# GpSimd arithmetic moved to VectorE in the Hyena and attention layers, and unsplit F32 side tasks in the first feed forward

## Chip, cores and metric

One core of a Trainium2 chip runs the whole program. The metric is the device time of one execution in microseconds, as the median of several runs. One more execution was taken by the hardware profiler, and every row below is from that one.

## What is computed

Two blocks follow each other on 256 tokens of width 1024, in F32. The first block has two layers; each is a hybrid mixer (stick-breaking attention, sparse attention with a top-k index, and a gated recurrence) and a feed forward of width 4096. The second block has two layers as well: a Hyena layer, an attention layer, each joined with a cross attention to a memory of 256 rows, and after each a mixture of 16 experts. Cut to the parts that the change touches:

```python
def second_block(x, mem, ...):
    mem_n = rms_norm_2(mem, mem_norm_g)
    for i in range(DEPTH):
        u = rms_norm_2(h, mix_norm_g[i])
        if i % N_MIXERS == 0:
            k_taps = hyena_filters(T, w1, b1, w2, b2, w3, freq)
            k_fft = jnp.fft.rfft(k_taps, axis=0)
            main = hyena_mixer(main_in, short_w, k_fft, skip)
        else:
            q = apply_axial_rope(rms_norm_2(q, at_q_norm_g[j]), cos, sin)
            kk = apply_axial_rope(rms_norm_2(kk, at_k_norm_g[j]), cos, sin)
            main = blocked_gqa(q, kk, vv)
        cross = memory_cross_attn(cq, mem_n, w_mem_kv[i])   # mem_n @ w_kv
        h = h + jnp.concatenate([main, cross], axis=-1) @ w_out[i]
        h = h + expert_choice_ffn(rms_norm_2(h, ffn_norm_g[i]), ...)
```

The Hyena filters (a small network with two sine layers, a third product with w3, a decay, a norm and a Fourier transform) and the memory's keys and values depend on no token, so the kernel makes them early, beside the first feed forward.

## The kernel before, in words

**Split products.** A weight tile or an activation is split into a high part (`hi`, rounded to F32R) and the rest (`lo`), and each product of two split operands is made of three F32R matmuls into one PSUM tile: `mm3`, lines 304 to 306. `split` (line 284) makes the parts of a weight tile: ScalarE copies `hi` (line 291), and the next engine of the cycle `lo_engines[0]` subtracts for `lo` (line 292). The cycle differs from stage to stage: VectorE alone in the mixers of the first block; `LO0 = (G, V)` in both feed forwards (`mlp`); `LO1 = (G, V)` in `hyena_layer`; `LO2 = (V, G, V)` in `attention_layer`, and `LO3 = (G, V)` for its output projection. `V` is VectorE, `S` ScalarE, `G` GpSimd, `PE` TensorE.

**Units and steps.** The dense work is a row of units (`dense_T`, `dense_M`, the closures in `mlp` and `out_second`). A unit first prepares (loads and splits a tile), two units ahead of its matmuls, and then runs: 24 matmuls of 256 columns or 12 of 512. `Pipe.feed` prepares and runs them in turn, and after each unit it takes every spawned task one step further, to its next `yield`. `Pipe.join` goes on until a given task has ended, with units as long as there are some. The instructions of each engine stand in one queue in an order that the framework's planner sets from its own costs.

**Weights.** `Ring.one` takes the next buffer and issues its transfer (line 187) on SP's queue. SP waits, in order, until the buffer's former content has been read. In the first block the ring has five buffers of 2048 elements a partition; later stages have other ones, and those of the experts become free as Hyena and attention release their own tiles.

**Side tasks of the first feed forward.** `mlp0_tasks` (line 1834) is spawned before `mlp(0, ...)` and joined before its last chunk. It runs `filters_task` (line 1063) and then `memory_task` (line 1161). `filters_task` makes `h1` and `h2` with `sin_layer`, keeps `h2` stacked as high and low part in `hst`, loads `w3` in four blocks, splits each block (`w3h`, `w3l`, line 1112 on GpSimd), makes two matmuls for each direction `d` (lines 1122 and 1123, of 128 and of 64 rows), multiplies by the decay (line 1124), sums absolute values on GpSimd (line 1130), makes sum and difference of the two directions, splits these (lines 1136 and 1137), and transforms them by `mm3` with the split Fourier matrix `Fh`, `Fl`. `memory_task` norms the memory with `Norm`, whose `half` (line 339) transposes on TensorE and splits the columns on ScalarE (line 347) and VectorE (line 348), and then makes keys and values for both layers by the helper `stream` over `dense_T` and `dense_M` units. These tasks end with 69 yields; the feed forward gives them some 62 units.

**Hyena.** `hyena_layer` (line 1309) feeds the projections `v`, `x1`, the cross query and `x2` (20 units), and spawns four tasks `chain(o, n)`: a Fourier transform, a complex product with the filter (lines 1371 to 1380; GpSimd has one of the two combinations, line 1375, and some of the `lo` parts), an inverse transform, and the gate. `short` (lines 1327 to 1334) makes the short convolution of a projection. `out_second` is the output projection, 16 units.

**Attention.** In `attention_layer` (line 1437), `rotate` multiplies by the sine table on GpSimd (line 1466) and by the cosine table on VectorE (line 1468). `attend` makes scores, softmax and values.

**Other lines named below.** 371 is the row norm's broadcast by matmul, from `nrb`; 801 and 1215 are F32 matmuls of the attentions; 1142 and 1143 are the filters' norm; 1352 is the transposition ahead of a Hyena chain; 360, 361 and 321 are small steps of a norm's inverse root on 128x2 elements.

```python
        S.activation(hi, src, AF.Copy)
        next(lo_engines[0]).tensor_tensor(lo, src, hi.bitcast(F32), op=ALU.subtract)
```

## Time and profile before

| what | value |
|---|---|
| runs: median (lowest to highest) | 1873.15 us (1870.21 to 1873.5) |
| the profiled execution: its time, its span | 1872.64 us, 1870.8 us |
| busy: TensorE matmuls, weight loads | 1628.8 us (87%), 1195.2 us (64%) |
| busy: VectorE, ScalarE, GpSimd | 985.2 us (53%), 676.6 us (36%), 315.1 us (17%) |
| moved by the transfers | 490.41 MB, mean 262 GB/s |

The span goes from the first to the last instruction. PE is TensorE (PEld its weight loads), DVE VectorE, ACT ScalarE, POOL GpSimd, SP the queue that issues nearly all transfers. L292 is line 292 of the kernel before. Shares of the whole span say little here, since the stages have different limits; so the rows below are by stage. Times in the views count from the span's start. Matmuls overlap, so that what one costs is read from the distance of two starts and not from its duration.

### The profile page before, as it was taken

Reading aid. Unit: us, or ns where it says so; the run is one execution under the profiler, and the core shown is the slowest. Engines: PE = TensorE matmul, PEld = TensorE weight load, DVE = VectorE, ACT = ScalarE, POOL = GpSimd, SP = SyncE. Lnnn points to the kernel's source line nnn. Section 1 sums busy time; section 2 is a strip of 40 time slices with the busy share of each in tenths; the row PEclk is TensorE's granted clock in tenths of the full one; section 3 lists DMA queues with packets and bytes.
Section 4 is the critical chain, followed back from the end, with each engine's and each line's share of the span. In section 5 each row is a group of like instructions: output and inputs, shape, how many; then the busy total and the mean of one; then the engine's idle time right before and its main releaser. Section 6 shows DMA issues by size and latency. Waiting matters only on the chain. (4 is left out here: it accounts for less than half of the span.)

```text
span 1870.8 us, 27208 instructions
## 1 busy us (share of the span) xinstructions
PE 1628.8 (87%) x11139; PEld 1195.2 (64%) x11139; DVE 985.2 (53%) x1740; ACT 676.6 (36%) x1118; POOL 315.1 (17%) x216
## 2 busy tenths in 40 slices
PE   8999999998999999999989988666667989776765
PEld 7998977788999989999878844212224655221221
DVE  6998686775579977645578752000006862110102
ACT  6446454554454555544445331000003652000001
POOL 1000026654300000444333300000002210000001
PEclk9999999999999999999999988898989999899888
DMA  7543564454644436755244689999998759999997
GB/s 257 160 137 125 172 201 160 164 203 161 209 142 147 130 124 203 278 185 196 99 153 157 254 353 425 425 426 424 426 405 315 272 203 401 425 425 425 425 421 274
DMA packets 136516, 490.41 MB, mean 262 GB/s; under 512 B 11153, under 2 KB 32068, under 8 KB 115912
## 3 DMA queue, kind: packets, MB, share of 16 engines
q1 hardware_dynamic: 135919, 488.11, 69.2%
q8 instruction: 87, 1.43, 0.3%
q10 hardware_dynamic: 472, 0.57, 0.1%
q14 instruction: 38, 0.30, 0.0%
HBM read 483.41 MB, written 5.24 MB: 261 GB/s over the span
## 5 line engine op out<-in xcount | busy, mean ns | idle before, releaser
L291 ACT ACTIVATE hi<-w 128x1024 fp32r<-128x1024 f32 (+3 forms) x330 | 328.0, 997 | 323.7 <-PE psT L306 162.3
L304 PE MATMUL psT<-xh,hi 128*128 128x256 f32 x1328 | 386.8, 291 | 0.9 <-ACT hi L291 0.9
L305 PE MATMUL psT<-xh,lo 128*128 128x256 f32 x1328 | 378.6, 285 | 4.6 <-POOL lo L292 2.7
L306 PE MATMUL psT<-xl,hi 128*128 128x256 f32 x1328 | 378.7, 285 | 0.0
L292 DVE TENSOR_TENSOR lo<-w,hi 128x1024 fp32r<-128x1024 f32 (+3 forms) x245 | 285.3, 1165 | 141.5 <-ACT hi L291 140.6
L292 POOL TENSOR_TENSOR lo<-w,hi 128x1024 fp32r<-128x1024 f32 (+1 forms) x85 | 205.0, 2413 | 590.2 <-ACT hi L291 584.6
L305 PEld LDWEIGHTS psT<-xh,lo 128*128 128x128 f32 x1328 | 256.4, 193 | 9.5 <-POOL lo L292 3.3
L304 PEld LDWEIGHTS psT<-xh,hi 128*128 128x128 f32 x1328 | 256.5, 193 | 9.2 <-issue 6.4
L306 PEld LDWEIGHTS psT<-xl,hi 128*128 128x128 f32 x1328 | 256.1, 193 | 1.4 <-issue 1.1
L1741 PE MATMUL psx<-w,late 128*32 128x256 f32 (+1 forms) x1024 | 154.4, 549 | 75.8 <-DMA w<-in_exp_w_gate 39.5
L1741 PEld LDWEIGHTS psx<-w,late 128*32 128x32 f32 x1024 | 47.1, 116 | 180.5 <-issue 74.9
L1741 PE MATMUL psx<-w,xg 128*32 128x256 f32 (+1 forms) x1024 | 124.3, 547 | 35.2 <-DMA w<-in_exp_w_up 19.7
L1793 PE MATMUL psy<-w,late 128*32 128x512 f32 x576 | 98.8, 601 | 33.7 <-DMA w<-in_exp_w_down 29.8
L1777 ACT ACTIVATE yy<-psy,rslot 128x512 fp32r<-128x512 f32 (+1 forms) x17 | 11.3, 662 | 320.6 <-PE psy L1793 253.7
L1741 PEld LDWEIGHTS psx<-w,xg 128*32 128x32 f32 x1024 | 40.5, 117 | 115.7 <-issue 60.6
L306 PE MATMUL acc<-lo,hh 128*128 128x512 f32 x256 | 100.8, 394 | 3.0 <-POOL lo L292 3.0
L305 PE MATMUL acc<-hi,hlo 128*128 128x512 f32 x256 | 100.8, 394 | 0.0
L304 PE MATMUL acc<-hi,hh 128*128 128x512 f32 x256 | 100.5, 392 | 0.0
L1778 DVE SCALAR_TENSOR_TENSOR yy<-psy,rslot,yy 128x512 fp32r<-128x512 f32 (+1 forms) x17 | 12.2, 720 | 162.0 <-ACT yy L1777 161.5
L1757 DVE TENSOR_TENSOR late<-late,psx 128x512 f32<-128x512 f32 (+1 forms) x16 | 8.1, 550 | 166.3 <-PE psx L1741 166.3
L1793 PEld LDWEIGHTS psy<-w,late 128*32 128x32 f32 x576 | 27.1, 110 | 101.1 <-DMA w<-in_exp_w_down 49.8
L1756 DVE SCALAR_TENSOR_TENSOR late<-psx,rslot,late 128x512 f32<-128x512 f32 (+1 forms) x16 | 9.1, 613 | 152.3 <-ACT late L1755 152.3
(495 smaller groups left out, 2850.1 us busy)
## 6 DMA issues: line engine op xcount, KB each, us to landing
w<-in_exp_w_gate SPq DMA_DIRECT2D x64, 1536.0 KB, 27.6
w<-in_exp_w_up SPq DMA_DIRECT2D x64, 1536.0 KB, 29.5
w<-in_exp_w_down SPq DMA_DIRECT2D x48, 1536.0 KB, 26.9
w<-in_w_in SPq DMA_DIRECT2D x39, 1024.0 KB, 5.2
w<-in_w_up SPq DMA_DIRECT2D x32, 1024.0 KB, 5.6
w<-in_w_down SPq DMA_DIRECT2D x32, 1024.0 KB, 7.1
w<-in_exp_w_down SPq DMA_DIRECT2D x18, 1024.0 KB, 14.2
w<-in_w_out SPq DMA_DIRECT2D x10, 1024.0 KB, 5.6
```

The source lines that it names most:

```text
L291: S.activation(hi, src, AF.Copy)
L292: next(lo_engines[0]).tensor_tensor(lo, src, hi.bitcast(F32), op=ALU.subtract)
L304: PE.matmul(ps, lh, rh, start=start, stop=False)
L305: PE.matmul(ps, ll, rh, start=False, stop=False)
L306: PE.matmul(ps, lh, rl, start=False, stop=stop)
L1741: mm = PE.matmul(pg[nm][n][32 * e:32 * e + 32, :c1 - c0], xg[gr // 2][:, k, 128 * (gr % 2) + 32 * e:128 * (gr % 2) + 32 * e + 32], wt[e][: ...
L1756: V.scalar_tensor_tensor(sg[:, :n], pg["gate"][i][:, :n], r2, sg[:, :n], op0=ALU.mult, op1=ALU.mult)
L1757: V.tensor_tensor(hid[:, c], sg[:, :n], pg["up"][i][:, :n], op=ALU.mult)
L1777: S.activation(yh, py, AF.Copy, scale=rs[:, 2, gr:gr + 1])
L1778: V.scalar_tensor_tensor(yl, py, rs[:, 2, gr:gr + 1], yh.bitcast(F32), op0=ALU.mult, op1=ALU.subtract)
L1793: PE.matmul(py[n][32 * e:32 * e + 32], hT[:, k, 32 * e:32 * e + 32], wt[e][:, k - k0, 512 * n:512 * n + 512], start=k == 0, stop=k == 5, t ...
```

## The change

The cycles `LO1`, `LO2` and `LO3` become VectorE alone, and the GpSimd instructions in `chain` and `rotate` go to VectorE; `LO0`, the cycle of both feed forwards, stays as it is. The side tasks use plain F32 operands in place of split ones: the memory's norm has a third form without `xl`; the memory's products read the weight tile of the ring; `filters_task` multiplies `h2` with `w3` by matmuls of 64 rows, one for each direction on its half of the rows, and transforms the unsplit sums.

```diff
@@ -277,9 +277,7 @@
     LO0 = (G, V)
-    LO1 = (G, V)
-    LO2 = (V, G, V)
-    LO3 = (G, V)
+    LO1 = LO2 = LO3 = (V,)
@@ -329,7 +327,10 @@
             self.src, self.g, self.ps = src, g, psum or B
-            if split:
+            self.x = None
+            if split is None:
+                self.x = pool.tile([128, 8, T], F32, name="xT")
+            elif split:
                 self.xh = (pool or xtp).tile([128, 8, T], F32R, tag="xh", name="xh")
@@ -344,6 +345,9 @@
                     k = k2 + j
+                    if self.x is not None:
+                        S.activation(self.x[:, k], ps[:, j], AF.Copy, scale=self.g[:, k:k + 1])
+                        continue
                     S.activation(self.xh[:, k], ps[:, j], AF.Copy, scale=self.g[:, k:k + 1])
@@ -1030,19 +1034,6 @@
...
-    def stream(units, pool):
...
@@ -1075,11 +1066,8 @@
             nc.sync.dma_start(dec, C["decay"])
-            raw = ring.one(C["fwd"]).rearrange("p t (s f) -> p t s f", s=2)[:, :, :, :128]
-            Fh = fp.tile([128, 2, 2, 128], F32R, name="fFh")
-            Fl = fp.tile([128, 2, 2, 128], F32R, name="fFl")
-            S.activation(Fh, raw, AF.Copy)
-            V.tensor_tensor(Fl, raw, Fh.bitcast(F32), op=ALU.subtract)
+            F = fp.tile([128, 2, 2, 128], F32, name="fF")
+            nc.sync.dma_start(F, C["fwd"].rearrange("p t (s f) -> p t s f", s=2)[:, :, :, :128])
             yield
@@ -1089,12 +1077,9 @@
             h2 = fp.tile([128, T], F32, name="fh2")
-            hst = fp.tile([128, T], F32R, name="fhst")
             ps = A("psf", [128, T])
...
             sin_layer(ps, fc[:, 1:2], fc[:, 2:3], h2, fp)
-            S.activation(hst, h2, AF.Copy)
-            V.tensor_tensor(hst[64:], h2[64:], hst[64:].bitcast(F32), op=ALU.subtract)
             ones = fp.tile([128, 2], F32, name="ones")
@@ -1103,25 +1088,22 @@
                     c = slice(384 * n, 384 * n + 384)
-                    w3 = fp.tile([128, 2, 384], F32, name="fw3")
+                    w3 = fp.tile([128, 384], F32, name="fw3", bufs=2)
                     for d in range(2):
-                        nc.sync.dma_start(w3[64 * d:64 * d + 64], I["hy_filt_w3_2"][0].rearrange("k (o d c) -> k o d c", o=2, d=2)[:, o, :, c])
-                    w3h = fp.tile([128, 2, 384], F32R, name="fw3h")
-                    w3l = fp.tile([64, 2, 384], F32R, name="fw3l")
-                    S.activation(w3h, w3, AF.Copy)
-                    G.tensor_tensor(w3l, w3[:64], w3h[:64].bitcast(F32), op=ALU.subtract)
-                    hs = {op: [fp.tile([128, 2, 384], F32R, tag=f"h{op}{i}", name="hs") for i in range(2)] for op in (ALU.add, ALU.subtract)}
+                        nc.sync.dma_start(w3[64 * d:64 * d + 64], I["hy_filt_w3_2"][0].rearrange("k (o d c) -> k o d c", o=2, d=2)[:, o, d, c])
+                    hs = {op: fp.tile([128, 2, 384], F32, tag=f"h{op}", name="hs") for op in (ALU.add, ALU.subtract)}
                     sab = fp.tile([128, 384], F32, tag="sab", name="sab")
...
                         hd = []
+                        sl = slice(t * 128, (t + 1) * 128)
+                        pd = [A("psf", [128, 384]) for _ in range(2)]
+                        for d in range(2):
+                            r = slice(64 * d, 64 * d + 64)
+                            PE.matmul(pd[d], h2[r, sl], w3[r], start=True, stop=True, tile_position=(64 * d, 0))
                         for d in range(2):
                             h = fp.tile([128, 384], F32, tag=f"hd{d}", name="hd")
-                            ps = A("psf", [128, 384])
-                            sl = slice(t * 128, (t + 1) * 128)
-                            PE.matmul(ps, hst[:, sl], w3h[:, d], start=True, stop=False)
-                            PE.matmul(ps, hst[:64, sl], w3l[:, d], start=False, stop=True)
-                            V.tensor_tensor(h, ps, dec[:, t, c], op=ALU.mult)
+                            V.tensor_tensor(h, pd[d], dec[:, t, c], op=ALU.mult)
                             if t == 0 and d == 0:
@@ -1131,10 +1113,7 @@
                         for op, dst in hs.items():
-                            x = fp.tile([128, 384], F32, tag="hx", name="hx")
-                            V.tensor_tensor(x, hd[0], hd[1], op=op)
-                            S.activation(dst[0][:, t], x, AF.Copy)
-                            G.tensor_tensor(dst[1][:, t], x, dst[0][:, t].bitcast(F32), op=ALU.subtract)
+                            V.tensor_tensor(dst[:, t], hd[0], hd[1], op=op)
                         yield
@@ -1147,7 +1126,7 @@
                         for t in range(2):
-                            mm3(pp[t], Fh[:, t, part], Fl[:, t, part], hs[op][0][:, t], hs[op][1][:, t], True, True)
+                            PE.matmul(pp[t], F[:, t, part], hs[op][:, t], start=True, stop=True)
                         S.activation(e, pp[0], AF.Copy)
@@ -1158,24 +1137,32 @@
-    def memory_task(ring, mp, sp, m, kvd):
-
-        nm = Norm(m, gain("mem_norm_g_2"), mp, A)
+    def memory_task(ring, mp, m, kvd):
+
+        nm = Norm(m, gain("mem_norm_g_2"), mp, A, None)
         yield from nm.task(lambda n: True)
...
             yield
-
-            def put_k(j, ps):
-                V.tensor_tensor(kv[:, 0], ps, nm.R[:, None, :].to_broadcast([128, 2, T]), op=ALU.mult)
-
-            def put_v(ps):
+            yield
+            ps = A("psT", [128, 2, T])
+            for i in range(2):
+                for q in range(2):
+                    for k in range(4):
+                        PE.matmul(ps[:, q], w[i][:, k, 128 * q:128 * q + 128], nm.x[:, 4 * i + k],
+                                  start=i == 0 and q == 0 and k == 0, stop=i == 1 and q == 1 and k == 3)
+                yield
+            V.tensor_tensor(kv[:, 0], ps, nm.R[:, None, :].to_broadcast([128, 2, T]), op=ALU.mult)
+            ps = [A("psM") for _ in range(2)]
+            for k0 in range(0, 8, 2):
                 for t in range(2):
-                    evac(kv[:, 1, t], ps[t][:, :256], t, nm.r[:, t:t + 1])
-
-            yield from stream(dense_T(ring, None, nm.xh, nm.xl, put_k, tiles=[x[:, :, :256] for x in w]), sp)
-            yield from stream(dense_M(ring, None, nm.xh, nm.xl, put_v, tiles=[x[:, :, 256:] for x in w]), sp)
+                    for k in (k0, k0 + 1):
+                        PE.matmul(ps[t][:, :256], nm.x[:, k, t * 128:(t + 1) * 128], w[k // 4][:, k % 4, 256:],
+                                  start=k == 0, stop=k == 7)
+                yield
+            for t in range(2):
+                evac(kv[:, 1, t], ps[t][:, :256], t, nm.r[:, t:t + 1])
             nc.sync.dma_start(kvd[l], kv)
@@ -1372,12 +1359,12 @@
                 V.tensor_tensor(a[3], pz[1], kf[:, f], op=ALU.mult)
-                G.tensor_tensor(a[0], a[0], a[1], op=ALU.subtract)
+                V.tensor_tensor(a[0], a[0], a[1], op=ALU.subtract)
                 V.tensor_tensor(a[2], a[2], a[3], op=ALU.add)
...
                     S.activation(yh[:, b], a[2 * part], AF.Copy)
-                    (G if part and not o else V).tensor_tensor(yl[:, b], a[2 * part], yh[:, b].bitcast(F32), op=ALU.subtract)
+                    V.tensor_tensor(yl[:, b], a[2 * part], yh[:, b].bitcast(F32), op=ALU.subtract)
                 yield
@@ -1398,7 +1385,7 @@
                     S.activation(ah[:, b], sz, AF.Copy)
-                    (V if n else G).tensor_tensor(al[:, b], sz, ah[:, b].bitcast(F32), op=ALU.subtract)
+                    V.tensor_tensor(al[:, b], sz, ah[:, b].bitcast(F32), op=ALU.subtract)
                     ready.add(("a", b))
@@ -1463,7 +1450,7 @@
                     for g in range(2):
-                        G.tensor_tensor(hx(rot[:, t, a:a + 64 * nh])[:, :, :, g], hx(qk[:, t, a:a + 64 * nh])[:, :, :, 1 - g],
+                        V.tensor_tensor(hx(rot[:, t, a:a + 64 * nh])[:, :, :, g], hx(qk[:, t, a:a + 64 * nh])[:, :, :, 1 - g],
                                         xhf(tg[:, j, t, 1])[:, None, :, g].to_broadcast([128, nh, 2, 16]), op=ALU.mult)
@@ -1833,12 +1820,12 @@
         yield from filters_task(ring, kd)
-        with tc.tile_pool(name="memp", bufs=1) as mp, tc.tile_pool(name="mems", bufs=3) as sp:
+        with tc.tile_pool(name="memp", bufs=1) as mp:
             m = mp.tile([128, 2, D], F32, name="mem")
...
                 yield
-            yield from memory_task(ring, mp, sp, m, kvd)
+            yield from memory_task(ring, mp, m, kvd)
     with ExitStack() as c1s:
```

## Rows read from the trace of the kernel before

**Rows 1.** By stage: length, busy PE, PEld, DVE, ACT, POOL; clock; DMA share; GB/s.
```profile
226.00:520.00 294.00, 276.03 (x1723) 242.20 (x1723) 199.58 (x256) 146.43 (x212) 136.36 (x75) 0.99 0.54 182
...
740.00:935.00 195.00, 194.99 (x1233) 176.39 (x1231) 109.30 (x126) 96.28 (x122) 77.76 (x33) 1.00 0.55 188
935.00:1084.00 149.00, 133.04 (x891) 121.47 (x890) 115.16 (x198) 67.79 (x130) 52.70 (x38) 0.98 0.56 201
1084.00:1405.00 321.00, 234.11 (x1577) 88.71 (x1577) 51.42 (x112) 29.08 (x55) 2.26 (x3) 0.91 0.99 412
1405.00:1545.00 140.00, 123.73 (x622) 79.48 (x626) 97.39 (x255) 70.75 (x165) 33.85 (x35) 0.93 0.69 259
```

**Rows 2.** Waits of TensorE, 226:520 us: in total, times, longest.
```profile
PE pst L344 <- DVE xl L348: 4.8, 1, 4.8
PE psf L304 <- DVE nrm L1143: 3.6, 4, 0.9
PE acc L306 <- POOL lo L292: 3.0, 4, 0.8
PE psf L1122 <- DVE fhst L1097: 2.1, 1, 2.1
PE psn L1142 <- POOL sab L1130: 2.1, 3, 0.9
PE psf L1094 <- ACT fh L1061: 2.0, 1, 2.0
```

**Rows 3.** Timeline of GpSimd, 936:948 us: start, duration, then the instruction.
```profile
936.12 4.96 POOL L292 TENSOR_TENSOR lo<-w,hi 128x1024 fp32r<-128x1024 f32 x2 [8.96 <-ACT hi L291]
```

**Rows 4.** Timeline of VectorE, 936:948 us.
```profile
936.54 2.19 DVE L360 TENSOR_TENSOR ms<-ss 128x2 f32<-128x2 f32 x1
938.77 2.33 DVE L361 TENSOR_SCALAR ms<-ms 128x2 f32<-128x2 f32 x1
...
941.41 0.16 DVE L321 TENSOR_TENSOR rt<-rh,nr 128x2 f32<-128x2 f32 x1
941.49 1.22 DVE L292 TENSOR_TENSOR lo<-w,hi 128x1024 fp32r<-128x1024 f32 x1
```

**Rows 5.** By ten us, columns as in rows 1.
```profile
260.00:270.00 10.00, 7.96 (x51) 7.17 (x51) 9.26 (x24) 5.40 (x7) 4.23 (x2) 0.83 0.50 145
...
950.00:960.00 10.00, 9.74 (x67) 9.54 (x67) 3.89 (x5) 2.92 (x4) 1.79 (x1) 0.83 0.64 206
```

**Rows 6.** Timeline of TensorE, 307.4:309.3 us: split products.
```profile
307.58 0.28 PE L306 MATMUL psT<-xl,hi 128*128 128x256 f32 x1
307.70 0.34 PE L1122 MATMUL psf<-fw3h,fhst 128*128 128x384 f32 x1
307.97 0.44 PE L1123 MATMUL psf<-fw3l,fhst 64*128 64x384 f32 x1
...
309.07 0.38 PE L304 MATMUL psT<-xh,hi 128*128 128x256 f32 x1
```

**Rows 7.** Timeline of TensorE, 667.8:668.5 us: an unsplit product.
```profile
667.91 0.60 PE L801 MATMUL psz<-skbd,sqT 128*128 128x256 f32 x2
668.34 0.27 PE L802 MATMUL psz<-future_eqb,negI 128*128 128x256 bf16 x1
```

**Rows 8.** Timeline of TensorE, 1465:1466 us: products on halves of the columns.
```profile
1464.94 1.09 PE L1215 MATMUL psv<-pT,mvv 128*64 128x256 f32 x8
1465.96 0.39 PE L304 MATMUL psM<-hi,xh 128*128 128x256 f32 x1
```

**Rows 9.** Waits of TensorE, 935:1084 us.
```profile
PE psr L371 <- DVE nrb L366: 3.3, 1, 3.3
...
PE pst L1352 <- DVE uv L1334: 2.6, 2, 1.9
...
PE psT L305 <- POOL lo L292: 1.3, 1, 1.3
```

**Rows 10.** Waits of TensorE, 1405:1545 us.
```profile
PE psT L305 <- POOL lo L292: 1.4, 1, 1.4
```

More of the change, by code (lines that the diff above doesn't have):

```diff
@@ L1031, in wait @@
             yield
-    def stream(units, pool):
-        ahead = deque()
-        for u in units + [None, None]:
-            if u:
-                hl.append(pool)
-                u.prep()
-                hl.pop()
-                ahead.append(u)
-            if len(ahead) == 3 or not u:
-                ahead.popleft().run()
-            yield
     def sin_layer(ps, b, fr, out, pool):
```

## The prediction

> **What bounds the kernel now.** I read the profile in five steps. First the busy times by stage [rows 1]. The reader is to see four kinds of stage. From 226 to 520 us (output projection and feed forward of the first layer, with the side tasks) TensorE is busy 276 of 294 us: its work is time, and 18 us are holes. From 740 to 935 us (the second feed forward) it is busy 194.99 of 195 us. In Hyena (935 to 1084 us) and around attention (1405 to 1545 us) TensorE has 16 us of holes in each, and VectorE is busy 115 of 149 and 97 of 140 us. In the experts between them the transfers are busy 0.99 of the time.
>
> Second, who ended TensorE's waits in the first feed forward [rows 2]: VectorE, GpSimd and ScalarE, six groups, 17.6 us. Third, why these engines are late [rows 3, 4]: GpSimd makes two differences of 128x1024 from 936.12 us on, 2.5 us each, and VectorE's two instructions on 128x2 elements that fall into them take 2.19 and 2.33 us; one on 128x2 after them, at 941.41, takes 0.16. VectorE makes a difference of 128x1024 itself in 1.22 us. So GpSimd's arithmetic is not beside VectorE's: in those 4.96 us it stopped VectorE's queue, which is in order, for some 4.2. Fourth, the clock [rows 5]: 0.83 granted from 260 to 270 us, just after the wait on fh, is 3.4 us of ten at 1.2 instead of 2.4 GHz, 1.7 us of work lost; 0.83 stands in Hyena too, at 950 to 960 and again in the next ten, and 0.86 at 430 to 440 after the wait on xl. Fifth, what a product costs on TensorE [rows 6, 7], used below.
>
> **The change, part by part.**
>
> *Side tasks, TensorE.* A split product is three instructions; one of 256 columns starts 0.12 us after the one before [rows 6], so the product costs 0.36 us. An unsplit one in F32 is two instructions in the trace: the 256-column pair at 667.91 holds TensorE until 668.34, 0.43 us [rows 7]. Unsplit costs more here, by 0.07 us. Memory keys and values are 2 layers x 32 products: 64 x 0.07 = **+4.5 us**. The filters' Fourier products are 16 of 384 columns, each 1.5 x 0.36 = 0.54 split and 1.5 x 0.43 = 0.65 unsplit: 16 x 0.11 = **+1.8**. The w3 products now take 1.37 us for four instructions (307.70 to 309.07 [rows 6]), 8 x 1.37 = 11.0: 128 and 64 rows alternate, and an instruction costs 0.37 where its columns alone are 0.18. Afterwards they are 16 unsplit products of 64 rows, in pairs on the two halves of the rows. One after another: 16 x 0.65 = 10.4, and eight changes of the row count at 0.19, 1.5: 11.9, a loss of 0.9. Side by side: 5.2 + 1.5 = 6.7, a gain of 4.3. The nearest row has products on two halves of the columns: eight such instructions of 256 columns take 1.02 us [rows 8], where eight on the whole array take 4 x 0.43 = 1.7. So I take **-4.3**. TensorE's work: +2.0 us.
>
> Two rules bear on these terms. The Trainium skill, "FP8 and Floating Point Precision", TensorE Precision Notes, says that true FP32 takes four passes through the array. By it, at 0.12 us a pass, the memory part would be +7.7 and not +4.5; the measured pair, 0.43 instead of 0.48, decides. The Trainium skill, "TensorE: Matmul & The Clock Gate", in the table under "Why this matters for your kernels", says that matmuls on distinct row groups run concurrently. By it the w3 pairs would come out at the lower end; no row of this trace shows row groups.
>
> *Side tasks, waits* [rows 2]. The units of this stage keep their cycle of GpSimd and VectorE, so GpSimd goes on stopping VectorE; only the side tasks' own arithmetic leaves both. L344 on xl (4.8): the memory norm's VectorE half disappears, ScalarE alone frees the PSUM tiles and is next late: 4.8 gone. L1122 on fhst (2.1): this copy and difference are gone, h2 is ready at once: 2.1. acc on GpSimd's lo (3.0) and psn on sab (2.1): the sum stays on GpSimd and so does lo, but no w3l and no hs queue before them, nor before ScalarE's single buffer of absolute values: I take two thirds, 3.4. L1094 on fh (2.0): the sine's chain is stopped by one w3l, which goes, and by lo's, which stay: half, 1.0. nrm (3.6): its instructions stay: 0. Gone: 4.8 + 2.1 + 3.4 + 1.0 = 11.3, and 1.7 for the slow stretch of the clock after the wait on xl; the one after fh I keep. Nothing new comes to VectorE or ScalarE here.
>
> *Side tasks, queues.* The steps fall from 69 to 63 yields, against some 62 units; a step with no unit over it is matmuls either way: 0. SP issues one transfer for F instead of a ring tile, and w3 in half the bytes with two buffers, where it waited for GpSimd's fw3l. The memory weights stay in the ring until matmuls have read them, and these wait for the landing itself, two steps after the issue; TensorE's next unit is queued behind them, SP's next weights behind the two ring tiles. SP runs tiles ahead, so I take 0; the bound is a step for each layer, a unit of 24 x 0.12 = 2.9 us: +5.8.
>
> First feed forward: 2.0 - 11.3 - 1.7 = **-11.0 us**. Ends: -18, if 2.6 of nrm, the rest of the 17.6 and both slow stretches go (2.0 - 2.6 - 14.0 - 3.4); +6.1, if only xl and fhst go (6.9), w3 runs in series (5.2), both landings are late (5.8) and both slow stretches stay (2.0 - 6.9 + 5.2 + 5.8).
>
> *Second feed forward.* Not touched by the diff, and without a hole in TensorE [rows 1]: **0**.
>
> *Hyena.* GpSimd's 52.7 us [rows 1], nearly all arithmetic (10 lo, 8 hl, 15 smaller), become half of that, 26 us, on VectorE. In return its stops go: 0.85 of GpSimd's time in the head (4.2 of 4.96), and I estimate 0.4 over the stage, since not every VectorE instruction is stopped: 21 us. VectorE's load so goes from 115 to 120 of 149; what changes is that the row-norm and short-convolution chains no longer stand still. Of [rows 9] I count nrb (3.3), GpSimd's lo (1.3) and the longest of uv (1.9) as gone, and two slow clocks (3.4); I add 1 for the load: 3.3 + 1.3 + 1.9 + 3.4 - 1 = **-9** (ends -14 and 0). The experts' transfers start as Hyena frees its tiles and then run at 0.99; a shorter Hyena moves them forward whole.
>
> *Attention.* GpSimd has 29 of its 33.9 us to give (two memsets and the router stay): 14 on VectorE, 12 of stops less by the same 0.4. The wait on lo goes (1.4 [rows 10]); eight hl differences enter the softmax part, where they may hold its reductions up. I take **-1** (-4 to +4).
>
> Sum: -11.0 + 0 - 9 - 1 = -21.0. The profiled execution took 1872.6 us (span 1870.8 and 1.8 around it), 0.5 under the median of the runs. 1872.6 - 21.0 = **1851.6 us**.
>
> **Rivals.** *Only the side tasks pay.* VectorE in Hyena swaps stops for work of its own, and the holes come back behind other instructions. For: its load falls by nothing in my own sum. Against: the 128x2 instructions stand in the row-norm chain that TensorE waits for [rows 4, 9]. 1872.6 - 11.0 = 1861.6 us.
>
> *The unsplit products eat the side tasks' gain.* With w3 in series (5.2) and late landings (5.8) the side tasks come to -11.0 + 11.0 = 0; with -10 from Hyena and attention 1862.6 us. For: unsplit is dearer by the rows [rows 6, 7]. Against: the memory weights' landing has the ring's lead.
>
> *Slower: VectorE becomes the bound in Hyena and attention.* If its instructions are long for another reason than GpSimd, nothing is given back: Hyena needs 115 + 26 = 141 us of VectorE, at the present share of 77% a stage of 183, +34; attention 97 + 14 at 70%, 159, +19. Half of that where chains wait, +26, less 11.0: 1888 us. It decides once VectorE's load in Hyena passes the 133 us for which TensorE is busy. For: TensorE waits there mostly on VectorE [rows 9]. Against: two elements in a row cannot take 2.19 us by themselves [rows 4].
>
> *It doesn't do what it says.* The waits may move to other instructions in the new order of the queues; the second feed forward shows GpSimd doing no harm where TensorE is full. +2.0 for the products and some 4 us of waits less: 1871 us, no change.
>
> **Numbers.** Chances: the forecast 0.60; only the side tasks 0.14; the gain eaten 0.12; no change 0.07; slower 0.07. 0.2% is 3.7 us, about what a measurement can tell. Faster by more: 0.60 + 0.14 + 0.12 = 0.86; within: 0.07; slower: 0.07. The range goes from the three lower ends together (-18 - 14 - 4 = -36, 1837) past the second and third case (1862) to 1866, a little short of the side tasks' upper end with Hyena and attention as forecast (6.1 - 10 = -3.9, 1868.7), which needs every miss at once.
>
> **What would show it.** Right: TensorE's waits from 226 to 520 us fall to some 6 us, none on xl or fhst, while the side matmuls take some 2 us more; in Hyena no 128x2 instruction of VectorE takes over 0.3 us; Hyena ends some 20 us earlier than now. Wrong: the two w3 products of a pair start 0.6 us apart; TensorE waits for in_w_mem_kv; VectorE is over 90% busy through Hyena; or the expert stages grow by what was won before them.

## The result, and the profile after

The changed kernel takes 1830.5 us (median of 4 runs, 1829.9 to 1832.0), the kernel before beside it 1873.3 us: a ratio of 0.9776 (95% interval 0.976 to 0.9793), 42.8 us faster. The forecast was 21 us faster, and 1830.5 lies below its range. The profiled execution took 1830.5 us, of which 1828.7 are its span.

Three stages hold the gain; what lies ahead of them and between them changed by less than 1 us each. I measure each between two products that both kernels have: the first feed forward with its output projection from that projection's first product to the last product of the feed forward, Hyena from there (in the second layer) to its last output product, and the stretch from the first expert product to attention's first scores.

| stretch | before, us | after, us | difference | forecast |
|---|---|---|---|---|
| first feed forward | 277.1 | 257.3 | -19.8 | -11.0 |
| second feed forward | 204.8 | 204.9 | 0 | 0 |
| Hyena | 150.0 | 131.7 | -18.3 | -9 |
| experts to attention's scores | 375.2 | 368.9 | -6.3 | } -1 |
| the rest to the end | 394.5 | 395.8 | +1.3 | } |

The busy time by stage of the kernel after answers to [rows 1]; the columns are the same.

```profile
226.00:500.00 274.00, 272.68 (x1645) 236.02 (x1643) 172.60 (x241) 127.97 (x179) 95.81 (x49) 1.00 0.57 192
720.00:915.00 195.00, 194.98 (x1233) 176.50 (x1232) 112.03 (x126) 95.67 (x120) 77.75 (x33) 1.00 0.56 188
915.00:1046.00 131.00, 128.53 (x893) 118.17 (x892) 113.11 (x228) 68.54 (x129) 1.46 (x5) 1.00 0.64 229
1046.00:1363.00 317.00, 233.17 (x1572) 87.37 (x1570) 49.99 (x112) 28.21 (x54) 2.12 (x3) 0.91 0.99 412
1363.00:1503.00 140.00, 125.69 (x640) 78.89 (x636) 101.61 (x283) 71.88 (x167) 5.49 (x10) 0.92 0.73 272
```

TensorE's holes in the first stage fall from 18.0 to 1.3 us and in Hyena from 16.0 to 2.5, and the granted clock is 1.00 in both. In Hyena GpSimd goes from 52.70 to 1.46 us of work, all of it now VectorE's, and yet VectorE's busy time falls, from 115.16 to 113.11 us. In the first feed forward GpSimd keeps 95.81 us, the units' differences and the sums of absolute values.

TensorE's waits after, first from 226 to 500 us [rows 2], then from 915 to 1047 us [rows 9]: in total, times, longest.

```profile
PE psf L1129 <- DVE nrm L1122: 0.7, 1, 0.7
PE psr L375 <- DVE nrb L370: 0.3, 1, 0.3
PE psf L1081 <- ACT fh L1052: 0.3, 1, 0.3
...
PE pst L345 <- DVE X L998: 0.6, 1, 0.6
PE psy L302 <- ACT yh L1366: 0.5, 1, 0.5
```

Of the 17.6 us of [rows 2] 1.0 is left, on nrm and fh; the wait on nrb stood there before too, with the same 0.3. In Hyena no wait is over 0.6 us.

VectorE's timeline in Hyena's head shows why. The row-norm's two instructions that took 2.19 and 2.33 us beside GpSimd [rows 4] are these:

```profile
917.04 3.49 DVE L290 TENSOR_TENSOR lo<-w,hi 128x1024 fp32r<-128x1024 f32 x3
...
921.23 0.15 DVE L364 TENSOR_TENSOR ms<-ss 128x2 f32<-128x2 f32 x1
...
923.28 0.16 DVE L365 TENSOR_SCALAR ms<-ms 128x2 f32<-128x2 f32 x1
```

They take 0.15 and 0.16 us, and VectorE makes three differences of 128x1024 in 3.49 us, where GpSimd made two in 4.96 [rows 3].

The prices of products, from TensorE's timeline after: a pair of w3 products (its four records, then the next unit's first), and four unsplit memory products (eight records) with the two that follow.

```profile
300.36 0.92 PE L1103 MATMUL psf<-fw,fh 64*128 64x384 f32 x4
301.20 0.39 PE L302 MATMUL psT<-xh,hi 128*128 128x256 f32 x1
...
433.45 1.89 PE L1161 MATMUL psM<-w,xT 128*128 128x256 f32 x8
434.99 0.58 PE L302 MATMUL acc<-hi,hh 128*128 128x512 f32 x1
435.41 0.39 PE L303 MATMUL acc<-hi,hlo 128*128 128x512 f32 x1
```

A w3 pair holds TensorE from 300.36 to 301.20, 0.84 us, where the four split instructions of [rows 6] took 1.37. Four memory products take 1.54 us, and the split product behind them costs 0.42 instead of the usual 0.23: with that return, 0.43 us a product, what [rows 7] gave.

Around attention the waits on GpSimd's lo [rows 10], on cqT and on qp are gone, and these stand at the head of the list (1363 to 1503 us):

```profile
PE psM L302 <- ACT hi L289: 5.0, 1, 5.0
PE psa L1605 <- DVE aff L1602: 2.6, 1, 2.6
PE pss L1768 <- ACT yy L1764: 1.6, 2, 0.8
PE pst L1194 <- ACT p L785: 1.0, 1, 1.0
```

The first was 3.8 us before, and the two others that are gone were these:

```profile
PE psl L1197 <- DVE cqT L1546: 2.5, 1, 2.5
PE pst L1501 <- DVE qp L1493: 1.7, 2, 1.4
```

ScalarE's hi there starts behind the landing of attention's first weights, which queue behind the experts' transfers.

### The profile page after: what moved, and what is told of

It reads as the page before. It is cut to its first block, busy times and chain, and to the rows that moved or that the text cites. A ratio compares the mean times of both kernels' runs of the same rounds, so it can differ in the third digit from the quotient of the medians.

```text
span 1828.7 us, 26929 instructions
## 1 busy us (share of the span) xinstructions
PE 1617.8 (88%) x11059; PEld 1182.6 (65%) x11059; DVE 960.5 (53%) x1782; ACT 657.9 (36%) x1084; POOL 194.8 (11%) x132
## 4 chain that ended last, share of the span: by engine, by line
PE 60%; DMA 30%; DVE 6%; ACT 2%; issue 1%; SPq 1%; DVEq 0%; ACTq 0%
DMA w<-in_exp_w_up 10%; DMA w<-in_exp_w_gate 10%; DMA w<-in_exp_w_down 9%; PE psT L302 8%; PE psT L303 8%; PE psT L304 8%; PE acc L302 3%; PE acc L303 3%; PE acc L304 3%; PE psM L302 3%; PE psx L1728 3%; PE psM L303 2%; PE psM L304 2%; DVE lo L290 1%; SPq L187 1%
## 5 line engine op out<-in xcount | busy, mean ns | idle before, releaser
L289 ACT ACTIVATE hi<-w 128x1024 fp32r<-128x1024 f32 (+3 forms) x318 | 319.7, 1006 | 359.9 <-PE psT L304 160.3
L302 PE MATMUL psT<-xh,hi 128*128 128x256 f32 x1296 | 376.4, 291 | 1.2 <-ACT hi L289 1.2
L290 DVE TENSOR_TENSOR lo<-w,hi 128x1024 fp32r<-128x1024 f32 (+3 forms) x254 | 291.6, 1150 | 147.2 <-ACT hi L289 146.3
L303 PE MATMUL psT<-xh,lo 128*128 128x256 f32 x1296 | 366.9, 283 | 1.2 <-DVE lo L290 1.2
L304 PE MATMUL psT<-xl,hi 128*128 128x256 f32 x1296 | 366.3, 283 | 0.0
L302 PEld LDWEIGHTS psT<-xh,hi 128*128 128x128 f32 x1296 | 247.7, 191 | 11.9 <-issue 8.5
L303 PEld LDWEIGHTS psT<-xh,lo 128*128 128x128 f32 x1296 | 248.0, 191 | 5.8 <-DVE lo L290 1.9
L304 PEld LDWEIGHTS psT<-xl,hi 128*128 128x128 f32 x1296 | 247.5, 191 | 0.8 <-issue 0.7
L290 POOL TENSOR_TENSOR lo<-w,hi 128x1024 fp32r<-128x1024 f32 x64 | 156.2, 2440 | 235.8 <-ACT hi L289 233.4
L1764 ACT ACTIVATE yy<-psy,rslot 128x512 fp32r<-128x512 f32 (+1 forms) x17 | 11.3, 662 | 318.8 <-PE psy L1780 251.1
L302 PE MATMUL acc<-hi,hh 128*128 128x512 f32 x256 | 104.5, 408 | 0.0
```

The lines of the kernel that those rows point to most:

```text
L302: PE.matmul(ps, lh, rh, start=start, stop=False)
L303: PE.matmul(ps, ll, rh, start=False, stop=False)
L304: PE.matmul(ps, lh, rl, start=False, stop=stop)
L1764: S.activation(yh, py, AF.Copy, scale=rs[:, 2, gr:gr + 1])
```

## The experiments

Times are medians, and each ratio is to the kernel before on the same chip; the three stretches are those of the table above, from each run's profile.

| run | us | ratio (95%) | first FF | Hyena | to scores |
|---|---|---|---|---|---|
| before | 1871.97 to 1873.33 | 1 | 277.1 | 150.0 | 375.2 |
| after | 1830.50 | 0.9776 (0.976 to 0.9793) | 257.3 | 131.7 | 368.9 |
| e1 | 1853.64 | 0.9902 (0.9885 to 0.9918) | 257.2 | 147.0 | 375.7 |
| e2 | 1854.95 | 0.991 (0.9895 to 0.9925) | 276.8 | 131.7 | 374.7 |
| e3 | 1868.41 | 0.9976 (0.9966 to 0.9985) | 277.7 | 148.9 | 368.5 |
| e4 | 1847.70 | 0.9872 (0.9857 to 0.9886) | 257.3 | 148.0 | 368.2 |
| e5 | 1867.15 | 0.9975 (0.9965 to 0.9986) | 270.2 | 147.3 | 375.8 |
| e6 | 1872.26 | 1.0 (0.999 to 1.001) | 276.3 | 148.6 | 373.7 |
| e7 | 1860.96 | 0.9941 (0.9927 to 0.9956) | 278.0 | 134.7 | 375.2 |
| e8 | 1829.12 | 0.977 (0.9755 to 0.9785) | 255.9 | 131.6 | 370.2 |
| e9 | 1825.59 | 0.9744 (0.9728 to 0.9761) | 251.5 | 131.7 | 370.0 |
| e10 | 1865.85 | 0.9961 (0.9946 to 0.9975) | 276.9 | 146.8 | 367.7 |
| e11 | 1836.56 | 0.9809 (0.9788 to 0.9829) | 257.3 | 136.0 | 367.8 |
| e12 | 1829.58 | 0.9766 (0.9746 to 0.9785) | 258.4 | 131.7 | 369.0 |

One thing is read off the table at once: wherever GpSimd still works in Hyena and nothing there was edited (before, e1, e3, e5, e6, e10), the stage takes 146.8 to 150.0 us, from one profiled execution to the next; without GpSimd it takes 131.6 or 131.7 every time. The profiled execution of before was at the upper end, so that Hyena's own gain is 15 to 18 us.

### Do the parts add up? (e1, e2, e3)

e1 has the side tasks alone: the changed kernel with the mixing layers' edits undone.

```diff
-    LO1 = LO2 = LO3 = (V,)
+    LO1 = (G, V)
+    LO2 = (V, G, V)
+    LO3 = (G, V)
...
-                V.tensor_tensor(a[0], a[0], a[1], op=ALU.subtract)
+                G.tensor_tensor(a[0], a[0], a[1], op=ALU.subtract)
```

> Only the side tasks of the first feed forward are changed; Hyena and attention keep GpSimd. Theory (the three parts add up, each in its own stage): the stage from the output projection to the last acc product is 19 to 20 us shorter, as in the full change, Hyena keeps its 149 us, total 1873 - 20 = 1853 us. Rival (a part of the 20 us needs the mixing layers' change, because all of them share GpSimd's queue order): 1860 us or more. The terms on record would give 1862.

e2 has Hyena alone (LO1 and the chains' three differences), on the kernel before.

```diff
-    LO1 = (G, V)
+    LO1 = (V,)
...
-                    (V if n else G).tensor_tensor(al[:, b], sz, ah[:, b].bitcast(F32), op=ALU.subtract)
+                    V.tensor_tensor(al[:, b], sz, ah[:, b].bitcast(F32), op=ALU.subtract)
```

> Only Hyena's split differences and its chains go to VectorE. Theory (parts add up): Hyena 18 us shorter, total 1873 - 18 = 1855 us, and TensorE's waits from the end of the second feed forward to Hyena's end fall from 16 to some 3 us. Rival (VectorE's relief is only part of it, and the expert stage behind gives some back): 1864 us, the 9 us that the forecast counted.

e3 has attention with its output projection alone; the router, which the expectation names, is not edited and keeps its differences on GpSimd.

```diff
-    LO2 = (V, G, V)
-    LO3 = (G, V)
+    LO2 = LO3 = (V,)
...
-                        G.tensor_tensor(hx(rot[:, t, a:a + 64 * nh])[:, :, :, g],
+                        V.tensor_tensor(hx(rot[:, t, a:a + 64 * nh])[:, :, :, g],
```

> Only attention's and the router's differences and the rotation go to VectorE. Theory (the 5 us between the first layer's experts and attention's scores are attention's own: waits on GpSimd's lo, on cqT and on qp and two slow stretches of the clock): 1873 - 5 = 1868 us. Rival (they come from transfers that start earlier behind a shorter Hyena): 1872 to 1873 us.

Against 1873.29 us the three give 19.7, 18.3 and 4.9 us, together 42.9, and the full change 42.8. The stretches say the same: each part shortens its own stretch, and of the other two only Hyena moves by over 1 us, by the variation just named. The theory holds, and the rivals fall: nothing of the side tasks' gain needs the mixing layers, and attention's 5 us are its own.

### Is it GpSimd's running, or waiting for its results? (e4, e11)

```diff
+        if idle[0] and next(idle[0]):
+            for k in range(shape[1] if len(shape) == 3 else 2):
+                beside(hi[:, k] if len(shape) == 3 else hi[:, 256 * k:256 * k + 256])
...
+    def beside(x):
+        G.tensor_tensor(scr[0][:, :x.shape[1]], x.bitcast(F32), x.bitcast(F32), op=ALU.subtract)
```

The first three lines run at every second split in Hyena, and beside is called behind the chains' differences too, in all as many elements as GpSimd had before (the expectation left eight of the instructions out).

> The changed kernel, with GpSimd subtracting again in Hyena, about as often and as much as before but for the eight differences of products (some 45 of its 52 us), into a scratch tile that nobody reads; no result waits for GpSimd. Theory (GpSimd's running instructions stop VectorE's queue, whoever needs them): VectorE's short instructions take 2 us again where they fall into them, Hyena grows by 8 to 16 us, total 1838 to 1847 us. Rival (what cost was waiting for GpSimd's slow results): Hyena within 2 us of the changed kernel, total 1830 to 1833 us.

e4 takes 1847.7 us, 17.2 more than the changed kernel, and Hyena is back at 148.0 us, although no instruction takes a result from GpSimd and all other engines together wait 0.4 us for it, once, to have a tile back. The theory holds, a little above its band. GpSimd's work came to 66.8 us, where the same elements took it 51.7 before and the expectation had 45. The smaller pieces are not the reason: a piece of 128x256 takes 0.61 us when nothing stops it, and four of them what one difference of 128x1024 took. Some take up to 1.71, since VectorE stops GpSimd as well, as rows below show. VectorE's groups, first after, then e4: busy and mean ns of one behind the bar.

```profile
L290 DVE TENSOR_TENSOR lo<-w,hi 128x1024 fp32r<-128x1024 f32 x20 | 24.2, 1221 | 1.3 <-ACT hi L289 1.3
L1367 DVE TENSOR_TENSOR yl<-ya,yh 128x384 fp32r<-128x384 f32 x16 | 8.3, 553 | 0.4 <-ACT yh L1366 0.4
...
L1358 DVE TENSOR_TENSOR ya<-psz,kf 128x384 f32<-128x384 f32 x8 | 4.4, 553 | 0.0
```

```profile
L291 DVE TENSOR_TENSOR lo<-w,hi 128x1024 fp32r<-128x1024 f32 x20 | 26.7, 1341 | 0.9 <-ACT hi L290 0.9
L1375 DVE TENSOR_TENSOR yl<-ya,yh 128x384 fp32r<-128x384 f32 x16 | 15.3, 993 | 0.4 <-ACT yh L1374 0.4
...
L1367 DVE TENSOR_TENSOR ya<-psz,kf 128x384 f32<-128x384 f32 x8 | 4.4, 547 | 0.4 <-PE psz L311 0.4
```

The same instruction on 128x384 goes from 553 to 993 ns where both operands are in SBUF (ya, yh), and stays at 553 and 547 where one is in PSUM (psz). The means alone don't show that GpSimd was running: it was beside 15 of the 16 instructions on yl, but beside 7 of the 32 on psz (four lines, the last of which is shown). So here are both kinds with GpSimd's pieces between them:

```profile
926.48 1.21 DVE L291 TENSOR_TENSOR lo<-w,hi 128x1024 fp32r<-128x1024 f32 x1
926.62 1.54 POOL L298 TENSOR_TENSOR pad<-hi 128x256 f32<-128x256 f32 x1
927.62 0.57 DVE L317 TENSOR_SCALAR nr<-ms 128x2 int32<-128x2 int32 x1
...
955.73 0.55 DVE L1367 TENSOR_TENSOR ya<-psz,kf 128x384 f32<-128x384 f32 x1
955.89 0.61 POOL L298 TENSOR_TENSOR pad<-hi 128x256 f32<-128x256 f32 x1
956.19 0.54 DVE L1368 TENSOR_TENSOR ya<-psz,kf 128x384 f32<-128x384 f32 x1
956.58 0.61 POOL L298 TENSOR_TENSOR pad<-hi 128x256 f32<-128x256 f32 x1
```

GpSimd's piece of 926.62 starts under VectorE's difference and takes 1.54 us; VectorE's next instruction, on 128x2 elements of another tile, then stands until that piece ends (928.16) and ends itself at 928.19. The products with psz run at 0.54 and 0.55 us over pieces that take their 0.61: neither stops the other. In the kernel before, 19 of the 32 ran while GpSimd did, at 548 ns on average. So it is not a general slowing of VectorE. One detail of the expectation was wrong: no instruction from and to 128x2 elements took 2 us; the longest was 0.58, because a piece that nothing stops runs for 0.61 us, where GpSimd's difference before ran for some 2.5. In these rows, as in [rows 3, 4], a stop ends with the other engine's instruction.

The Trainium skill, "SBUF — State Buffer", section "Who interferes with whom", says that VectorE and GpSimd share a pair of ports, that the one to come second is blocked until the other's instruction ends, and that a VectorE instruction with at most one SBUF input, outside its two-port modes, does not contend. Both halves agree with these rows: the stop at 927.62 ends 0.03 us behind GpSimd's instruction, and the products with psz aren't stopped.

e11 is e4 with copies in place of the subtractions.

```diff
-        G.tensor_tensor(scr[0][:, :x.shape[1]], x.bitcast(F32), x.bitcast(F32), op=ALU.subtract)
+        G.tensor_copy(scr[0][:, :x.shape[1]], x.bitcast(F32))
```

> The changed kernel with GpSimd in Hyena copying the same tiles into the scratch tile, where the earlier run subtracted them: one operand in SBUF instead of two, as many instructions, nobody waits. Theory (any GpSimd arithmetic that reads SBUF stops VectorE for as long as it runs): Hyena grows in proportion to GpSimd's time in it, which at 0.4 to 0.7 us a copy is 30 to 45 us against 67; half of the 17 us, total 1836 to 1842 us. Rival (two operands are what VectorE is stopped by): within 2 us of the changed kernel, 1830 to 1833 us.

1836.56 us, 6 more than the changed kernel: the low end of the theory's band, outside the rival's. The intervals of the two ratios still overlap, so the stage is the better witness: 136.0 us against 131.7. Hyena's stage in e4 (916 to 1064 us) and e11 (915 to 1051 us), columns as in [rows 1]:

```profile
916.00:1064.00 148.00, 134.49 (x896) 120.49 (x895) 134.46 (x230) 68.92 (x130) 68.32 (x76) 0.99 0.55 196
```

```profile
915.00:1051.00 136.00, 130.50 (x896) 118.76 (x895) 121.23 (x230) 69.27 (x130) 51.58 (x76) 1.00 0.60 214
```

Against 113.11 us without GpSimd, VectorE is busy 21 us more beside 68 us of subtractions and 8 more beside 52 of copies, 0.31 and 0.16 of GpSimd's time. One operand stops VectorE too (the instruction on yl takes 756 ns on average, where it took 553 and 993), but the stage grows by 4 us and not by half of 16: what it costs is not in proportion to GpSimd's time, which itself holds the time for which VectorE stopped GpSimd.

### Which part of Hyena, which of attention? (e7, e10)

e7 changes in Hyena only the cycle of the weights' differences, `LO1 = (G, V)` to `LO1 = (V,)`, on the kernel before.

> The kernel before with Hyena's differences of weights alone on VectorE (18 instructions, some 35 of GpSimd's 52.7 us); the chains' differences stay on GpSimd. Theory (what counts is GpSimd's time beside VectorE): two thirds of Hyena's 18 us, 12, in the head of the stage (nrb, uv, lo and two slow stretches of the clock), total 1861 us, the waits on ux and yh stay. Rival (what counts is the length of the chains, of which GpSimd's small differences are links): 5 us or less, 1868 us.

1861.0 us and Hyena 134.7: 12 to 15 of the stage's 15 to 18 us, as the theory had it. Its remark on the waits was half wrong. The longest of those that are left, from 937 to 1074 us:

```profile
PE psy L304 <- ACT yh L1379: 1.5, 2, 0.9
PE pst L344 <- DVE X L994: 0.6, 1, 0.6
```

The wait on yh stays, at 1.5 instead of 2.1 us, but the 3.0 us on ux went though the chains were not touched.

e10 moves the weights' differences in attention and its output projection (`LO2 = LO3 = (V,)`) and leaves the rotation on GpSimd.

> Of the attention part only the weights' differences go to VectorE; the rotation (twelve instructions, 8.4 us) stays on GpSimd. Theory (the differences, 20.5 us of GpSimd's time, give most): from the first layer's experts to attention's scores 4 of the 6 to 7 us, the wait on lo and one on cqT gone, the wait on qp stays; total 1870 us. Rival (the rotation holds the scores up, since it is a link of their chain): 1 us or less in that stretch, 1872 to 1873 us.

The stretch to the scores takes 367.7 us, with the rotation moved as well (e3) 368.5: the differences give all of it and the rotation nothing, and the wait on qp is gone too. The total, 1865.85, is below e3's, but the intervals overlap, and the profiles spread the difference over stretches that neither edits: 2.1 us are in Hyena (146.8 against 148.9) and 2.2 behind the scores (396.4 against 398.6).

### What pays in the first feed forward? (e5, e6, e8, e9, e12)

e5 keeps every product of the side tasks split and moves only the filters' differences from GpSimd to VectorE.

```diff
-                    G.tensor_tensor(w3l, w3[:64], w3h[:64].bitcast(F32), op=ALU.subtract)
+                    V.tensor_tensor(w3l, w3[:64], w3h[:64].bitcast(F32), op=ALU.subtract)
...
-                            G.tensor_tensor(dst[1][:, t], x, dst[0][:, t].bitcast(F32), op=ALU.subtract)
+                            V.tensor_tensor(dst[1][:, t], x, dst[0][:, t].bitcast(F32), op=ALU.subtract)
```

> The kernel before, with the filters' differences (of w3 and of the sums of filters) on VectorE instead of GpSimd and everything still split. Theory (in the first feed forward too it is GpSimd's arithmetic that makes the waits, by stopping VectorE and by queueing lo and sab): the waits of the filters' part (fh, fhst in part, lo, sab, nrm, about 12 us with the slow clock after fh) mostly go although no product is changed, total 1862 to 1865 us; the wait on xl stays. Rival (the unsplit chain is what pays, since copies and differences are no longer waited for): 1870 to 1873 us.

1867.15 us, between the two; the stage gives 6.9 of its 19.8 us. Its waits:

```profile
PE pst L344 <- DVE xl L348: 4.8, 1, 4.8
PE psf L304 <- DVE nrm L1143: 2.8, 3, 1.1
PE psf L1094 <- ACT fh L1061: 2.5, 1, 2.5
PE psf L1122 <- DVE fhst L1097: 1.4, 1, 1.4
PE acc L306 <- POOL lo L292: 0.4, 1, 0.4
```

The sab and most of the lo waits are gone; fh, nrm and fhst stay. This alone spoke for the rival, that unsplitting is what pays.

e6 has the memory part's new code (unsplit keys and values, and a norm that doesn't split its columns) on the kernel before, filters untouched:

```diff
-        nm = Norm(m, gain("mem_norm_g_2"), mp, A)
+        nm = Norm(m, gain("mem_norm_g_2"), mp, A, None)
```

> The kernel before with the memory part alone unsplit; filters, Hyena and attention as before. Theory (the wait on xl with its slow clock goes, 4.8 + 1.7, and the 64 unsplit products cost 4.5 to 5.5 more): 1 to 2 us faster, 1871 to 1872 us, so that 18 of the side tasks' 20 us are the filters'. Rival (the memory differences on GpSimd and VectorE also delayed the units' lo, and half of the side tasks' gain is here): 1863 us.

1872.26 us, no difference that can be told from noise (the interval is 2 us wide on either side). The wait on xl is gone and the side products cost more, but a new one takes part of its place, `acc` on VectorE's lo:

```profile
PE psf L1128 <- DVE fhst L1103: 2.1, 1, 2.1
...
PE psf L1100 <- ACT fh L1067: 2.0, 1, 2.0
PE acc L306 <- DVE lo L292: 1.7, 1, 1.7
```

So by itself the memory part is worth 2 us at the most, and the rival's 1863 is out.

e8 is the changed kernel with `LO0 = (V,)`, both feed forwards' differences on VectorE, and the sum of absolute values too.

> The changed kernel with both feed forwards' differences and the sum of absolute values on VectorE too. Theory (TensorE has holes of 1.3 us left in the first feed forward and none in the second, so GpSimd stops VectorE there at no cost): 1829 to 1832 us, no change. Rival (VectorE's short instructions gain as in Hyena): 1826 us or less. Other rival (VectorE, now with 64 more differences of 1.2 us, comes late): over 1834 us.

1829.1 us, no measurable change, as the theory had it: in these two stages, where TensorE has no holes left, GpSimd beside VectorE costs nothing. VectorE isn't late either.

e9 is e8 with the memory part as it was before, split, with its differences on VectorE by e8's `LO0`.

> The version without GpSimd in the feed forwards, with the memory products split again as before (their differences on VectorE). Theory (an unsplit product with the return to split ones costs 0.43 us against 0.36, and the wait on xl came from GpSimd's two differences beside the memory norm): 4 to 5 us faster than that version, about 1825 us, no wait on xl over 1 us. Rival (VectorE's sixteen more differences and the norm's xl hold TensorE up by as much): 1829 us or more.

1825.6 us, as expected, and no wait on xl or anything else. The stage takes 251.5 us against e8's 255.9: -4.4, and 64 x (0.43 - 0.36) = 4.5. The intervals of the two total times overlap, so it is the stage that shows it. The stage up to the last product, 226 to 483 us, columns as in [rows 1], is TensorE's from end to end:

```profile
226.00:483.00 257.00, 256.92 (x1622) 224.15 (x1621) 181.27 (x279) 131.91 (x182) 0.10 (x1) 1.00 0.57 197
```

e12 is e9 with the filters split again too, their differences on VectorE as in e5: every product of this stage is then as it was before the change, and GpSimd does no arithmetic in it.

> The version of the run before (no GpSimd in the feed forwards, memory split) with the filters split again as well, all their differences on VectorE: nothing is unsplit and GpSimd does no arithmetic in this layer. Theory (unsplitting the filters pays by itself, since it takes copies and differences out of the chains to fh, fhst and the sums and puts two w3 products side by side: about 12 us by the difference of the runs so far): 1836 to 1838 us, with TensorE waiting on fhst and fh again. Rival (these waits were long only because GpSimd's lo stopped VectorE beside them; what is left is -4.3 for w3, +1.6 for the Fourier products and the wait on fhst): 5 us or less, 1828 to 1831 us.

1829.58 us, the rival's number: the time of the changed kernel, with no product of the side tasks unsplit. Its waits from 226 to 500 us:

```profile
PE acc L302 <- ACT hi L289: 1.7, 1, 1.7
PE psr L375 <- DVE nrb L370: 0.3, 1, 0.3
```

Nothing waits on fh, fhst, nrm, sab, xl or lo. By the stage e12 is 6.9 us behind e9 (258.4 against 251.5), more than the rival's 5. Some 2 of them are the prices of the products; the rest is the one wait of 1.7 us in the list and the clock behind it, granted at 0.50 from 278 to 282 us and at 0.64 from 282 to 286, an estimated 3.4 us of work. So e5's reading fell: those waits were long because GpSimd's remaining work, the units' differences above all, stopped VectorE beside the side tasks. Taking GpSimd out of this stage gives 18.7 us of it (277.1 to 258.4) with the products as they were; unsplitting the side tasks and leaving the units on GpSimd gives 19.8; both together, with the memory split as its prices want it, 25.6. The two are mostly two ways to the same waits.

## Why the prediction was too cautious

The sign, the place and the mechanism were right, and the likeliest case came: the side tasks and Hyena both pay, the second feed forward doesn't move, the experts' transfers move forward whole. None of the rivals occurred; VectorE in Hyena is busy 113 of 131 us and never the bound. The error is in three sums of waits, all on the same side. One reason was too narrow: the waits on xl and fhst went, as forecast, but e12 shows them gone with every product split, as soon as GpSimd does nothing in this stage.

**First feed forward, -11.0 against -19.8.** The products came out as worked: memory 64 x 0.07 (0.43 against 0.36), w3 8 x (0.84 - 1.37) = -4.2 where -4.3 was forecast, the Fourier products about +2. A w3 pair takes 0.84 us; two unsplit Fourier products, as wide but on all rows and one after the other, take 1.08 (four records from 288.25 to 289.33). The Trainium skill, "TensorE: Matmul & The Clock Gate", table under "Why this matters for your kernels", says that matmuls on distinct row groups run concurrently. This trace agrees in part: in seven of the eight pairs the two products start within 0.01 us of each other, but 0.84 us is neither 0.54, the time of one Fourier product, nor 1.08. Landings were not late; TensorE waits for no memory weight.

What failed is the step "*Side tasks, waits*", in its shares: "nrm (3.6): its instructions stay: 0", "half" of fh, "two thirds" of lo and sab, and with them "the one after fh I keep" of the clock. Measured, 16.6 us of the 17.6 went instead of 11.3, and both half-clock stretches, some 3.4 us instead of 1.7. That is 7.0 of the 8.8 us missed. Most of the rest may be a cost that the list of waits doesn't carry: the wait on fh stands there with 2.0 us, but the products on its two sides start 2.33 us apart where the usual distance is 0.12. At some 0.2 us for each of a dozen waits that would be 2 us more, an estimate from this one wait.

The shares were wrong for one reason. I kept a wait when the late instruction itself was kept. But nrm, fh and the rest were late by the queue ahead of them, and that queue moves as a whole. The sine's stretch shows it for fh, first before, then after. For the other waits this isn't traced; that e12 has none of them, with all their instructions kept, speaks for it.

```profile
259.98 1.88 POOL L1112 TENSOR_TENSOR fw3l<-fw,fw3h 64x768 fp32r<-64x768 f32 x1 [2.48 <-ACT fw3h L1111]
260.04 1.84 DVE L312 TENSOR_SCALAR nr<-ms 128x2 int32<-128x2 int32 x1
264.71 0.42 ACT L1061 ACTIVATE fh<-sa 64x256 f32<-64x256 f32 x1 [2.20 <-DVE sa L1060]
...
261.04 0.15 DVE L310 TENSOR_SCALAR nr<-ms 128x2 int32<-128x2 int32 x1
263.55 0.42 ACT L1052 ACTIVATE fh<-sa 64x256 f32<-64x256 f32 x1 [1.15 <-DVE sa L1051]
```

VectorE's nr took 1.84 us beside fw3l, ahead of the sine's last steps, and takes 0.15 now. Counted from the stage's first product, which comes at 231.1 us before and at 231.8 after, fh starts 1.8 us earlier (31.8 instead of 33.6), while TensorE has run out of other work at the same 32.0 us; so the wait falls from 2.0 to 0.3. A wait that is the remainder of a race goes to zero as soon as the loser gains that much.

**Hyena, -9 against -18.3.** The step "Of [rows 9] I count nrb (3.3), GpSimd's lo (1.3) and the longest of uv (1.9) as gone" took 6.5 of 16 us of holes; 13.5 went, those on ux (3.0), yh (2.1, now 0.5) and VectorE's own lo (1.0) with them; the first two stood so in the list before:

```profile
PE pst L1352 <- DVE ux L1404: 3.0, 3, 1.5
...
PE psy L304 <- ACT yh L1379: 2.1, 2, 1.4
```

Both half-clock stretches went, as forecast (3.4). "I add 1 for the load" should have been a gain: by the rows after, GpSimd's former instructions take VectorE 10 x 1.22 + 8 x 0.69 + 12 x 0.55 + 3 x some 0.4 = 25.5 us (26 forecast), and its busy time still fell by 2, so that the stops had been 27.5 us, 0.53 of GpSimd's 51.7 us and not the 0.4 that I estimated. e4 shows the same in reverse. Up to 3 us of the difference may be the profiled execution of before, whose Hyena was a long one; e2's own total, 18.3 us below, doesn't show it.

**Attention, -1 against -5.** Beside the lo wait (1.4 [rows 10]) those on cqT (2.5) and qp (1.7) went, which the sum left out, and two half-clock stretches (granted 0.91 in 1445 to 1465 and 1465 to 1485 us before, 1.00 after). ScalarE's p (1.6) and a longer wait on hi, 5.0 after 3.8, give some back, and so does the clock around that wait: granted 0.90 from 1405 to 1425 us before, 0.68 from 1363 to 1383 after. Whether the hl differences in the softmax "may hold its reductions up" isn't settled: the waits on p, which the list of before doesn't have, come from the softmax, and no run tells the two apart.

**The range.** Its lower end, -36, was the three lower ends of the stages together (-18, -14, -4). All three were passed. For the first stage that end kept 1 us of nrm and left out the restart cost; for Hyena it was set by the waits that I could explain one by one.

## What to carry to other kernels

If two engines stop each other, don't price a move between them by the durations in the profile: those of the receiving engine are partly the giver's doing, and here VectorE took over 25 us of work and was busy for less. Behind an in-order engine that feeds the bound, count the holes as one sum with a common cause, with the half clock (1.7 us) and the restart (0.2 us) that a wait can carry, and not wait by wait by its last instruction. And where a change holds two remedies for the same waits, try either one alone: here unsplit products were worth keeping for the filters (6.9 us of the stage, of which some 2 by their prices) and not for the memory (-4.4).

## What was not expected of the hardware

Four things. VectorE's instructions with an operand in PSUM kept their duration beside GpSimd (548 ns on average for the 19 before that ran while it did, 0.54 and 0.55 us in e4), while equal ones from SBUF took 993 in e4. VectorE stops GpSimd too: a piece of 0.61 us took 1.54 under a difference of VectorE's. GpSimd's copies stopped VectorE less for each us that they ran than its subtractions did (0.16 against 0.31). And an unsplit F32 product is cheaper in a row than the pair of [rows 7] made it look (0.385 us), but the first split product behind a row pays 0.19 us, so that short rows cost as forecast.

What stays open: why Hyena with GpSimd in it varies by 3 us between kernels that don't edit it. The traces show where: TensorE's idle time in the stage goes from 12.0 us (e10, without the wait on nrb) to 16.3 (e3), and the granted clock is 0.97 in e10, 0.98 in before and e6, and 0.99 in e1, e3 and e5. Why a wait falls into one execution and not into another, no run looked into.
